# Twelve V columns as six pairs of block products, with two head chains and overlapping scan chunks, in a hybrid Mamba-2 and dilated-attention block

## The chip, the cores and the metric

The kernel runs on one core of a Trainium2 chip. The metric is device time in microseconds (us) of one execution; the figure given for a kernel is the median of its runs. TensorE (PE) multiplies, VectorE (DVE), ScalarE (ACT) and GpSimd (POOL) do the elementwise work, and all transfers are issued by SyncE (SP), one after the other. Each engine takes its own instructions in order.

## The reference

One layer over x of 1024 tokens by 1024 features:

```python
h = rmsnorm(x, norm_mix);  proj = h @ w_in          # z, xBC, dt, q/k/v, gate logits
y_ssm = mamba2_branch(z, xBC, dt, ...) @ w_ssm_out  # conv, silu, chunked scan: 32 heads in 4 groups, 8 chunks of 128
q, k = rope(q), rope(k)                             # 12 heads of 128, three patterns with strides 1, 4, 16
y_att = dilated_attention_branch(q, k, v) @ w_att_out   # softmax over the window, then over the three patterns
x = x + (sigmoid(g0) * y_ssm + sigmoid(g1) * y_att) @ w_mix_out
h = rmsnorm(x, norm_ffn)
x = x + (silu(h @ w_gate) * (h @ w_up)) @ w_down
return rmsnorm(x, norm_final)
```

In the scan a chunk's output needs the state that all chunks before it in its group leave; chunks of one group follow one another by that state alone. A head's attention output is divided and weighted only when the statistics of its three patterns are there.

## The kernel before, in words

**Numbers.** Every large product is made in float32 accuracy out of three float32r matmuls (`mm3`: high by high, high by low, low by high), each of 128x128 weights by 512 columns. A weight tile is loaded raw, ACT casts its high part, DVE subtracts for the low part.

**First stretch (to about 495 us).** z, x, B and C columns of `w_in` (40 columns of 128) are computed in pairs. A pair is a 2x2 block product, done with seven block products instead of eight (class `Seven`, object `A`): `prep` forms sums of weight blocks on POOL and splits each of the seven operands (`split`: ACT copy, DVE subtraction, 128x512); `unit` runs 7 x 4 x 3 = 84 matmuls; `chain` adds the products up on DVE (seven additions of 128x512 from PSUM) and hands two columns to their tasks (`xs_task`, `z_task`, ...), which write DRAM. The list `flat` merges "heavy" pairs (x, B and C: a convolution on DVE) with "light" ones (z).

**Second stretch (495 to about 1165 us).** The other columns go one by one (`direct`, `unit_a`): 2 x 8 x 3 = 48 matmuls, one weight split of 128x1024. They are 36 columns, k, q and v of 12 heads, then gates. Between these matmuls a recorded list of tasks puts the scan and the attention: `chunk(g, c)` for 4 groups by 8 chunks, `head_bg` for 12 heads, one after the other (`att_bg`), `quarter_task` after each two chunks (it writes the scan's output, sums squares with two one-column matmuls and so frees the slab that held X), and `q_load`, which brings X, Z and BC of the next two chunks from DRAM into three slabs of the pool `ssd` (six slabs: two quarters). In `q_load` BC is the last of the three and takes the slab that the quarter before last frees last. `combine(sp)` weights the outputs of six heads.

**Order.** `Pace` is a clock inside the builder: it holds a cost for each instruction and spreads the tasks' instructions among the PE stream when it takes their inputs to be due. It fixes the order on every engine; on the chip an instruction that comes too early in that order stalls its engine.

**Third stretch (from 1165 us).** With `merge` fired, the last five gates, then output projections (`mx_unit`), mixing, the FFN (again with `Seven`) and the down product. The change leaves it as it is, but for where two slabs and the scan's outputs come from.

Of the kernel before, what the change touches and what calls it, by code (L numbers as in the profile page):

```python
# [11 lines left out]
F32 = mybir.dt.float32  # L12
# [44 lines left out]
N_WTS = 7  # L57
N_BRIDGE = 3
N_FLAT_GATES = 0
N_SSD = 6  # L60
SLACK = 4.5
# [272 lines left out]
def hybrid_block(ctx, tc, x, norm_mix, w_in, b_gate, conv_w, conv_b, dt_bias, a_log, d_skip, ssm_norm,  # L334
# [126 lines left out]
    bc_d = [dr.tile([P, 4, 3, 256], F32, name=f"bc_d{g}") for g in range(NG)]  # L461
    b12_d = [dr.tile([P, 4, 512], F32, name=f"b12_d{i}") for i in range(2)]
# [353 lines left out]
    def chunk(g, c):  # L816
# [23 lines left out]
        if c > 0:  # L840
            eb = halves.get([P, 512])
            pair = ea_d[r0:r0 + HG, :].rearrange("(f e) l -> e f l", e=2)
            for e in range(2):
                nc.sync.dma_start(f4(eb.v)[e * 64:(e + 1) * 64], pair[e].partition_broadcast(64))
# [9 lines left out]
        nc.gpsimd.tensor_tensor(f4(y.v), xT, dcol[:, g * 4:(g + 1) * 4].unsqueeze(2).to_broadcast([P, 4, P]), ALU.mult)  # L854
        for h in range(HG):
            gh = g * HG + h
            nc.scalar.activation(E[:, h, :], E[:, h, :], AF.Relu, bias=dtv["acs"][:, c, gh:gh + 1], scale=-1.0)
        nc.scalar.activation(E, E, AF.Exp, scale=-1.0)
# [10 lines left out]
        if not last:  # L869
            yield [xw]  # L870
            yield from bank.room()
            pst = bank.get([P, 512])
            mm(pst.v, Btok, xw.v, True, True)
            xw.free()
            yield [pst, Sn]
            if c == 0:
                nc.vector.tensor_copy(Sn.v, pst.v)
            else:
                nc.vector.tensor_tensor(Sn.v, Sn.v, pst.v, ALU.add)
            pst.free()  # L880
        yield [E]
        nc.vector.tensor_tensor(E, E, cbm.unsqueeze(1).to_broadcast([P, HG, P]), ALU.mult)
        if c > 0:
            yield from bank.room()
            po = bank.get([P, 512])
            for f in range(4):
                fs = slice(f * P, (f + 1) * P)
                mm(po.v[:, fs], G["S"].v[:, fs], CT, True, True)
            G["S"].free()
# [32 lines left out]
    def quarter_task(g, q):  # L922
# [24 lines left out]
        yield [rs]  # L947
        yield from bank.room()
        yield from halves.room()
        pr, rT = bank.get([NCH, P]), halves.get([NCH, P])  # L950
# [6 lines left out]
        rT.free()  # L957
        pace.fire(f"ssd{g}")
# [99 lines left out]
    def rope_task(which, head, r, ps):  # L1058
# [5 lines left out]
        yield from slabs.room(3 if which else 2)  # L1064
        if which:
            att["U", head] = slabs.get([P, S])
# [21 lines left out]
    def v_task(head, r, ps):  # L1088
        yield from slabs.room(2)
        t, V = slabs.get([P, S]), slabs.get([P, 8, P])  # L1090
# [14 lines left out]
        att["v", head] = V  # L1105
        pace.fire(f"v{head}")

    def head_bg(sp, gi, i):
# [3 lines left out]
        yield f"v{head}"  # L1112
        yield [att[0, head], att[1, head], att["v", head]]
        q, k, v = att[0, head].v, att[1, head].v, att["v", head].v
        r = STRIDE[gi]
        if i == 0:
# [6 lines left out]
        for b0 in range(0, 8, step):  # L1123
            yield from bank.room()
            yield from halves.room()
            ps, scb = bank.get([P, 512]), halves.get([P, 512])
            sc = scb.v
# [32 lines left out]
            yield [sc]  # L1160
            yield from bank.room()
            yield from halves.room()
            pt, pT = bank.get([P, 512]), halves.get([P, 512])
# [6 lines left out]
            yield [pT]  # L1170
# [18 lines left out]
        for t in (att[0, head], att[1, head], att["v", head]):  # L1189
            t.free()  # L1190

    def stats_out(sp, gi):
# [7 lines left out]
        att["T", sp, gi] = tt  # L1200
        yield from bank.room()
        yield from halves.room()
        pt, sT = bank.get([32, P]), halves.get([32, P])
# [18 lines left out]
    def combine(sp):  # L1222
# [33 lines left out]
        for i in range(2):  # L1256
            slot = sp * 2 + i
            us = [att["U", gi * 4 + slot] for gi in range(3)]
            for gi in range(3):
                yield from eslabs.room()  # L1260
                fb = eslabs.get([P, S])
                nc.sync.dma_start(fb.v, fd[gi * 2 + i].partition_broadcast(P))
                yield [fb]
                eng = nc.gpsimd if gi < 2 else nc.vector
                eng.tensor_tensor(us[gi].v, us[gi].v, fb.v, ALU.mult)
                fb.free()
            yield [us[0], us[2]]
            nc.vector.tensor_tensor(us[0].v, us[0].v, us[2].v, ALU.add)
            us[2].free()
            yield [us[0], us[1]]  # L1270
            nc.vector.tensor_tensor(us[0].v, us[0].v, us[1].v, ALU.add)
            us[1].free()
            yield [us[0]]
            nc.sync.dma_start(att_d[slot], us[0].v)
            us[0].free()
        pace.fire(f"att{sp}")

    def att_bg():
        for sp in range(2):
            for gi in range(3):  # L1280
                for i in range(2):
                    yield from head_bg(sp, gi, i)
                pace.spawn(stats_out(sp, gi))
            pace.spawn(combine(sp))
# [37 lines left out]
    def direct(*a):  # L1322
# [3 lines left out]
        def run(ps=None, ths=(0, 1)):  # L1326
            ps = unit_a(lids, ps, ths)
            if 1 in ths:
# [6 lines left out]
    units = [direct(kind, gi, head) for sp in range(2) for gi in range(3)  # L1335
             for head in (gi * 4 + sp * 2, gi * 4 + sp * 2 + 1) for kind in "kqv"]
# [792 lines left out]
```

## Time and profile before

| | |
|---|---|
| runs | 2197.47, 2199.08, 2405.64 us; median 2199.08 |
| profiled execution | 2199.41 us, its span 2197.6 us |
| PE busy | 2146.8 us (98%), weight loads 1770.6 us (81%) |
| DVE, ACT, POOL busy | 1502.6 (68%), 885.9 (40%), 631.5 us (29%) |
| transferred | 299.83 MB, 136 GB/s on average |
| granted PE clock | 0.994 over the span |

How to read it: an engine's busy time says how much it did, not whether anybody waited for it. Where PE is busy all through a window, only its own work and its own waits set the time there; what the other engines do counts when PE's idle time names them. A matmul's row shows a modelled duration longer than the distance to the next start, so PE's rate is read from start to start.

### The profile page before, as it was taken

The page shows a single profiled execution, that of the slowest core. Times are in us where ns is not written, and L with a number is a line of the kernel's source. Part 1 is how long each engine was busy: PE and PEld are TensorE (multiplying, and loading weights), DVE is VectorE, ACT ScalarE, POOL GpSimd, SP SyncE. Part 2 cuts the span into 40 slices and gives each one's busy share as a digit, 9 for nine tenths or more (in the row PEclk, how much of TensorE's full clock was granted, in tenths as well). Part 3 has the DMA queues.
Part 4 walks back from the last instruction along what each step waited for, and adds up shares of the span by engine and source line. Part 5 has one row for each costly group of instructions (what it writes and reads, how often), then busy time and mean ns, then how long its engine had stood idle before and what let it go on. Part 6 is the DMA issues. An engine that isn't in the chain of part 4 may idle for free. (4 is left out here: it accounts for less than half of the span.)

```text
span 2197.6 us, 27736 instructions
## 1 busy us (share of the span) xinstructions
PE 2146.8 (98%) x10428; PEld 1770.6 (81%) x10428; DVE 1502.6 (68%) x2050; ACT 885.9 (40%) x1590; POOL 631.5 (29%) x406
## 2 busy tenths in 40 slices
PE   6999999999999999999999999999999999999996
PEld 6788878888888888888888887888778888888885
DVE  6698988885667777744424347644897777767787
ACT  4543443445555565443323224322333333324444
POOL 1332332213544544511012003001454544420002
PEclk9999999999999999999999999999999999999998
DMA  3534243446555554521246467364132323349332
GB/s 128 165 97 123 77 138 106 129 130 201 180 154 167 166 164 153 170 73 39 49 145 213 135 199 237 110 190 127 44 109 95 122 92 115 106 153 336 119 96 101
DMA packets 302602, 299.83 MB, mean 136 GB/s; under 512 B 20036, under 2 KB 246276, under 8 KB 302212
## 3 DMA queue, kind: packets, MB, share of 16 engines
q1 hardware_dynamic: 302468, 298.06, 43.5%
q8 instruction: 82, 1.34, 0.3%
q14 instruction: 52, 0.43, 0.1%
HBM read 225.00 MB, written 73.01 MB: 136 GB/s over the span
## 5 line engine op out<-in xcount | busy, mean ns | idle before, releaser
L166 POOL TENSOR_TENSOR xr<-xr,nfin 128x512 f32<-128x512 f32 x16 | 21.7, 1366 | 185.1 <-ACT jk L166 131.2
L166 POOL TENSOR_TENSOR slab__28_12063<-h2hi,h2lo 128x1024 f32<-128x1024 f32 x1 | 2.4, 2389 | 136.0 <-PE wide__54_11701 L166 136.0
L166 POOL TENSOR_TENSOR slab__26_10566<-slab__26_10566,last__2_10549 128x1024 f32<-128x1024 f32 x1 | 2.4, 2395 | 131.5 <-DMA slab__26_10566<-yt_d 131.5
L166 POOL TENSOR_TENSOR more__3_12059<-h2hi,h2lo 128x512 f32<-128x512 f32 x2 | 2.6, 1294 | 62.3 <-DVE h2lo L166 62.3
L166 POOL TENSOR_TENSOR slab__2_4015<-slab__2_4015,slab__3_4012 128x1024 f32<-128x1024 f32 x1 | 2.4, 2397 | 59.8 <-DMA slab__3_4012<-in_rope 59.8
L166 ACT ACTIVATE jk<-xr 128x512 f32<-128x512 f32 x16 | 10.1, 632 | 15.4 <-DVE xr L166 11.2
L166 POOL TENSOR_TENSOR slab__6_7169<-slab__6_7169,slab__30_9323 128x1024 f32<-128x1024 f32 x1 | 2.4, 2392 | 45.0 <-DMA slab__30_9323<-fd 45.0
L166 POOL TENSOR_TENSOR slab__2_620<-slab__2_618 128x512 f32<-128x512 f32 x1 | 4.0, 3991 | 37.6 <-DMA slab__2_618<-in_w_in 37.6
L166 PE MATMUL wide__1_184<-hhi,slab__1_248 128*128 128x256 f32 (+1 forms) x24 | 8.8, 367 | 2.6 <-ACT hhi L166 2.6
L166 PE MATMUL wide__1_184<-hlo,slab__1_248 128*128 128x256 f32 (+1 forms) x24 | 8.9, 371 | 2.3 <-DVE hlo L166 2.3
L166 DVE TENSOR_TENSOR slab__23_8663<-slab__23_8663,slab__31_9353 128x1024 f32<-128x1024 f32 x1 | 1.2, 1224 | 14.2 <-DMA slab__31_9353<-fd 14.2
L166 POOL TENSOR_TENSOR slab__53_15458<-slab__22_15150,slab__53_15271 128x512 f32<-128x512 f32 x1 | 1.3, 1305 | 32.1 <-DVE slab__53_15271 L166 32.1
L166 ACT ACTIVATE xr<-xr,or 128x512 f32<-128x512 f32 x8 | 5.6, 716 | 11.3 <-DVE or L166 11.3
L166 POOL TENSOR_TENSOR slab__1_596<-hhi,hlo 128x1024 f32<-128x1024 f32 x1 | 2.4, 2406 | 26.7 <-DVE hlo L166 26.7
L166 POOL TENSOR_TENSOR slab__9_8393<-slab__9_8393,slab__3_4012 128x1024 f32<-128x1024 f32 x1 | 2.4, 2403 | 26.5 <-ACT slab__9_8393 L166 26.5
L166 POOL TENSOR_TENSOR slab__21_8664<-slab__21_8664,slab__3_4012 128x1024 f32<-128x1024 f32 x1 | 2.4, 2393 | 25.6 <-ACT slab__21_8664 L166 25.6
L166 POOL TENSOR_TENSOR slab__11_8945<-slab__11_8945,slab__3_4012 128x1024 f32<-128x1024 f32 x1 | 2.4, 2391 | 24.6 <-ACT slab__11_8945 L166 24.6
L166 DVE TENSOR_TENSOR slab__33_9977<-slab__33_9947,slab__61_9976 128x512 fp32r<-128x512 f32 x1 | 0.7, 694 | 12.6 <-PE wide__45_9931 L166 12.6
L166 DVE TENSOR_TENSOR hlo<-slab__1_600,hhi 128x1024 fp32r<-128x1024 f32 x1 | 1.2, 1226 | 11.9 <-DMA slab__3_882<-in_w_in 11.9
L166 PE MATMUL bank__1_186<-ident 128*128 128x128 f32 x36 | 5.9, 343 | 2.7 <-DMA ident<-in_consts 2.7
L166 PEld LDWEIGHTS wide__1_184<-hhi,slab__1_248 128*128 128x128 f32 x24 | 5.3, 219 | 3.9 <-ACT hhi L166 3.7
L166 PEld LDWEIGHTS wide__1_184<-hlo,slab__1_248 128*128 128x128 f32 x24 | 5.3, 219 | 3.9 <-DVE hlo L166 3.8
(7646 smaller groups left out, 8262.7 us busy)
## 6 DMA issues: line engine op xcount, KB each, us to landing
xr<-x_d SPq DMA_DIRECT2D x8, 512.0 KB, 6.4
out<-xr SPq DMA_DIRECT2D x16, 256.0 KB, 2.1
b_d<-hhi SPq DMA_DIRECT2D x1, 1024.0 KB, 5.2
b_d<-hlo SPq DMA_DIRECT2D x1, 1024.0 KB
slab__1_150<-in_x SPq DMA_DIRECT2D x1, 512.0 KB, 3.8
slab__1_151<-in_x SPq DMA_DIRECT2D x1, 512.0 KB
slab__1_158<-in_norm_mix SPq DMA_DIRECT2D x1, 512.0 KB
slab__1_165<-in_w_in SPq DMA_DIRECT2D x1, 512.0 KB, 7.3
```

What stands on the lines that cost most here:

```text
L166: r = call(*args, **kw)
```

## The change

Six parts, in one edit:

1. The 12 V columns leave the list of single columns and become six light pairs of the first stretch (26 pairs instead of 20). `v_task` works in the pool `own`, and V goes to DRAM (`v_d`); `v_load` brings it back when its head starts.
2. Two chains of heads run side by side (`att_bg(0)`, `att_bg(1)`); a head's output U goes to DRAM (`u_d`) at its end, except for the last two, and `slot_bg` reads three of them back when the weights are there.
3. `chunk` asks for E late, takes fewer buffers at once, and starts the next chunk as soon as the state is updated, before its own output is finished.
4. Nine of the eleven gates follow the 24 k and q columns as fillers; two come after `merge` (five before).
5. The weight pool has six slabs instead of seven in the second stretch.
6. The scan's outputs are loaded from slabs as they come free (`y_load`, `spare`) instead of from the `ssd` pool and after `merge`.

```diff
+    v_d = [dr.tile([P, 8, P], F32, name=f"v_d{i}") for i in range(12)]
+    u_d = [dr.tile([P, S], F32, name=f"u_d{i}") for i in range(12)]
...
     def chunk(g, c):
...
-        yield [E, X, BC]
-        yield from halves.room(5)
-        y, xd = halves.get([P, 512]), halves.get([P, 512])
+        yield from halves.room(1 if last else 3)
+        xd = halves.get([P, 512])
         if not last:
             xw, Sn = halves.get([P, 512]), halves.get([P, 512])
...
+        yield [X, BC]
         yield from bank.room()
         pcb = bank.get([P, P])
         mm(pcb.v, BT, CT, True, True)
...
+        yield from halves.room(2 if c else 1)
+        y = halves.get([P, 512])
...
+        if not last:
+            G["S"] = Sn
+            pace.spawn(chunk(g, c + 1))
+        elif g + 1 < NG:
+            pace.spawn(chunk(g + 1, 0))
+        yield [E]
+        for h in range(HG):
...
-        if not last:
-            G["S"] = Sn
-            pace.spawn(chunk(g, c + 1))
-        elif g + 1 < NG:
-            pace.spawn(chunk(g + 1, 0))
         yield [E, xd]
...
     def v_task(head, r, ps):
-        yield from slabs.room(2)
-        t, V = slabs.get([P, S]), slabs.get([P, 8, P])
+        yield from own.room(2)
+        t, V = own.get([P, S]), own.get([P, 8, P])
...
-        att["v", head] = V
-        pace.fire(f"v{head}")
+        yield [V]
+        nc.sync.dma_start(v_d[head], V.v)
+        V.free()
+
+    def v_load(head):
+        yield from slabs.room()
+        t = att["v", head] = slabs.get([P, 8, P])
+        nc.sync.dma_start(t.v, v_d[head])
...
+        if (sp, gi) != (1, 2):
+            yield [att["U", head]]
+            nc.sync.dma_start(u_d[head], U)
+            att["U", head].free()
+        pace.fire(f"u{head}")
...
+    def slot_bg(sp, i):
...
+        for gi in range(3):
+            yield f"u{gi * 4 + slot}"
...
+            us.append(slabs.get([P, S]))
+            nc.sync.dma_start(us[gi].v, u_d[gi * 4 + slot])
+        yield f"fd{sp}"
+        for gi in range(3):
+            yield from slabs.room()
+            fb.append(slabs.get([P, S]))
+            nc.sync.dma_start(fb[gi].v, att["fd", sp][gi * 2 + i].partition_broadcast(P))
+        for gi in range(3):
+            yield [us[gi], fb[gi]]
+            eng = nc.gpsimd if gi < 1 else nc.vector
+            eng.tensor_tensor(us[gi].v, us[gi].v, fb[gi].v, ALU.mult)
+            fb[gi].free()
...
-    units = [direct(kind, gi, head) for sp in range(2) for gi in range(3)
-             for head in (gi * 4 + sp * 2, gi * 4 + sp * 2 + 1) for kind in "kqv"]
-    gates = [direct("gate", i) for i in range(2 + N_BRIDGE + N_FLAT_GATES, 16)]
+    columns = [(kind, gi, head) for sp in range(2) for gi in range(3)
+               for head in (gi * 4 + sp * 2, gi * 4 + sp * 2 + 1) for kind in "kq"]
+    gates = [("gate", i) for i in range(2 + N_BRIDGE + N_FLAT_GATES, 16)]
+    for i in range(len(gates) - N_LAST):
+        columns.insert(FIRST_GATE + i * GATE_STEP, gates.pop(0))
+    units, gates = [direct(*c) for c in columns], [direct(*c) for c in gates]
...
+    light += [(("v", h // 4, h), ("v", h // 4, h + 1)) for h in range(0, 12, 2)]
...
-            wts.pieces.extend(slabs.pieces.popleft() for _ in range(N_WTS))
+            wts.pieces.extend(slabs.pieces.popleft() for _ in range(N_WTS_B))
...
-    pace.spawn(att_bg())
+    for i in range(2):
+        pace.spawn(att_bg(i))
...
-    for u in units:
-        u()
-    while not pace.events.issuperset(("att1", "y01")):
-        if len(gates) > 5:
-            gates.pop(0)()
-        else:
-            pace.idle()
+    while units:
+        next_unit()
+    while not pace.events.issuperset(("fd1", "ssd3")):
+        pace.idle()
```

The diff does not say where `Pace` then puts things. Two places matter.

**PE, from the end of a quarter to the next quarter's first product.** The two one-column matmuls (`128x1`) are the quarter's sums of squares and the last reader of X's slab; the load of the next BC into that slab may go only then. The next chunk's first matmul reads that BC (`slab2__18_4431` before, `slab2__19_5515` now). Before, in group 0:

```order
L166 MATMUL bank2__49_4423<-slab7__1_143,slab2__17_4019 128x1 x2
L166 MATMUL bank3__49_4427<-half4__2_4382,slab18__3_4029 128x512
L166 MATMUL wide1__23_4202<-hhi_147,slab21__15_4058 128x512
L166 MATMUL wide1__23_4202<-hlo_148,slab21__15_4058 128x512
L166 MATMUL wide1__23_4202<-hhi_147,slab10__16_4059 128x512
L166 MATMUL wide1__23_4202<-hhi_147,slab21__15_4058 128x512
L166 MATMUL wide1__23_4202<-hlo_148,slab21__15_4058 128x512
L166 MATMUL wide1__23_4202<-hhi_147,slab10__16_4059 128x512
L166 MATMUL bank1__52_4444<-slab18__3_4029,half0__2_4295 128x128 x4
L166 MATMUL bank0__49_4328<-half7__2_4408,slab25__3_4212 128x128 x4
L166 MATMUL bank2__50_4455<-slab4__18_4378,half9__2_4381 64x128 x8
L166 MATMUL bank3__50_4473<-slab2__18_4431 128x128
```

and now, the corresponding place:

```order
L169 MATMUL bank3__63_5502<-slab7__1_167,slab2__18_5038 128x1 x2
L169 MATMUL bank0__68_5508<-slab15__3_5051,half6__2_5243 128x128 x4
L169 MATMUL wide0__30_5419<-hhi_171,slab12__21_5293 128x512
L169 MATMUL wide0__30_5419<-hlo_172,slab12__21_5293 128x512
L169 MATMUL wide0__30_5419<-hhi_171,slab27__20_5294 128x512
L169 MATMUL wide0__30_5419<-hhi_171,slab12__21_5293 128x512
L169 MATMUL wide0__30_5419<-hlo_172,slab12__21_5293 128x512
L169 MATMUL wide0__30_5419<-hhi_171,slab27__20_5294 128x512
L169 MATMUL bank2__67_5535<-slab5__20_5375,half2__2_5377 64x128 x8
L169 MATMUL bank1__69_5545<-ident_163,half4__3_5454 128x128 x4
L169 MATMUL bank3__64_5550<-slab2__19_5515 128x128
```

Between the sums and the matmul that reads BC stood a 128x512 float32 matmul, six matmuls of a column, eight of 128x128 and eight of 64x128; now a float32 matmul and four of the 128x128 are gone and four transposes (`ident`) have come in.

**SP, at the start of the second stretch.** `in_w_in` is a column's weights, `in_rope` the two rotation tables, then X, Z and BC of the first quarter; the bracket names the semaphores that the transfer waits for. Before:

```order
L166 DMA slab23__17_4008<-in_w_in 128x8x128 [waits DMAHW6_49,DMAHW5_49,Activation_49]
L166 DMA slab19__3_4010<-in_rope 128x1024 [waits PE_49]
L166 DMA slab16__3_4012<-in_rope 128x1024 [waits DMAHW7_49,PE_49]
L166 DMA slab2__17_4019<-xq_d0_117 128x1024 [waits DMAHW0_49,PE_49]
L166 DMA slab1__14_4020<-zq_d0_121 128x1024 [waits DMAHW1_49,PE_49]
L166 DMA slab11__15_4021<-bc_d0_125 128x768 [waits DMAHW2_49,PE_49]
```

and now:

```order
L169 DMA v_d11_140<-own0__24_4948 128x1024 [waits DMAHW4_49,Activation_49]
L169 DMA slab12__20_5028<-in_w_in 128x8x128 [waits DMAHW5_49,PE_49]
L169 DMA slab18__3_5030<-in_rope 128x1024 [waits DMAHW6_49]
L169 DMA slab19__3_5032<-in_rope 128x1024 [waits DMAHW7_49]
L169 DMA slab2__18_5038<-xq_d0_117 128x1024 [waits DMAHW0_49]
L169 DMA slab28__20_5039<-zq_d0_121 128x1024 [waits DMAHW1_49]
L169 DMA slab10__21_5040<-bc_d0_125 128x768 [waits DMAHW2_49]
```

The weight load ahead of the tables waited for ACT and for two transfers; now it waits for a transfer and for PE, and the matmul it waits for is the last one of the stretch's first column. The tables and the first quarter stand behind it.

## Rows read from the trace of the kernel before

**Rows 1.** The page, part 1: busy us (share of the span) xinstructions of each engine.

```profile
PE 2146.8 (98%) x10428; PEld 1770.6 (81%) x10428; DVE 1502.6 (68%) x2050; ACT 885.9 (40%) x1590; POOL 631.5 (29%) x406
```

**Rows 2.** Busy time by window: window, its length, busy us (xinstructions), clock, DMA share, GB/s.

```profile
60.00:495.00 435.00, 432.23 (x1925) 354.83 (x1924) 371.81 (x452) 185.65 (x282) 117.90 (x80) 1.00 0.40 121
495.00:1116.00 621.00, 619.72 (x3565) 510.92 (x3565) 382.32 (x549) 307.05 (x665) 227.71 (x150) 1.00 0.45 136
1165.00:2145.00 980.00, 967.56 (x4324) 799.49 (x4323) 655.85 (x819) 328.77 (x534) 251.09 (x152) 1.00 0.45 143
165.00:330.00 165.00, 162.23 (x729) 133.37 (x728) 147.70 (x188) 68.52 (x109) 47.91 (x35) 1.00 0.37 113
```

**Rows 3.** PE's waits over the whole span: us in total, times, longest us.

```profile
PE bank__23_2264 L166 <- DVE own__7_2108 L166: 1.6, 1, 1.6
...
PE bank__106_7798 L166 <- DVE slab__6_7169 L166: 0.8, 1, 0.8
```

**Rows 4.** Timeline of PE: start us, duration us, operation; 22 matmuls apart.

```profile
497.78 0.39 PE L166 MATMUL wide__22_3931<-hhi,slab__15_3830 128*128 128x512 f32 x1
...
502.77 0.39 PE L166 MATMUL wide__22_4001<-hhi,slab__13_3874 128*128 128x512 f32 x1
```

**Rows 5.** Timelines of DVE, ACT and POOL: one of each kind that the change adds.

```profile
489.90 0.68 DVE L166 TENSOR_TENSOR own__15_3866<-bank__42_3881,own__13_3777 128x512 f32<-128x512 f32 x1
485.12 1.22 DVE L166 TENSOR_TENSOR slab__15_3875<-slab__16_3795,slab__13_3874 128x1024 fp32r<-128x1024 f32 x1
474.84 0.59 ACT L166 COPY own__13_3777<-bank__43_3785 128x512 f32<-128x512 f32 x1 [3.50 <-PE bank__43_3785 L166]
```

**Rows 6.** Timeline of PE and SP between a quarter's sums and BC's first reader.

```profile
549.47 0.32 SPq L166 DMA_DIRECT2D slab__18_4431<-bc_d  x1
548.90 0.50 PE L166 MATMUL bank__49_4423<-slab__1_143,slab__17_4019 128*128 128x1 f32 x4
551.59 1.05 PE L166 MATMUL bank__52_4444<-slab__3_4029,half__2_4295 128*128 128x128 f32 x8
552.48 1.06 PE L166 MATMUL bank__49_4328<-half__2_4408,slab__3_4212 128*128 128x128 f32 x8
553.46 1.09 PE L166 MATMUL bank__50_4455<-slab__18_4378,half__2_4381 128*64 128x128 f32 x16
554.49 0.49 PE L166 MATMUL bank__50_4473<-slab__18_4431 128*128 128x128 f32 x2
554.81 0.60 PE L166 MATMUL bank__53_4475<-ident,slab__16_4429 128*128 128x128 f32 x4
555.36 1.13 PE L166 MATMUL bank__51_4494<-slab__3_4068,slab__3_4161 128*128 128x256 f32 x4
```

**Rows 7.** Tiles of three BC loads (at 549.5, 667.9 and 820.8 us): issue to landing.

```profile
DMA to landing us min/median/max: 3.3/3.3/3.3
DMA to landing us min/median/max: 6.5/6.5/6.5
DMA to landing us min/median/max: 7.6/7.6/7.6
```

**Rows 8.** Transfers issued from 495 to 505 us: KB each, us from issue to landing.

```profile
slab__3_4012<-in_rope SPq DMA_DIRECT2D x1, 512.0 KB, 6.1
...
slab__14_4020<-zq_d SPq DMA_DIRECT2D x1, 512.0 KB, 7.6
```

**Rows 9.** Timeline of POOL: the first rotation.

```profile
505.27 2.40 POOL L166 TENSOR_TENSOR slab__2_4015<-slab__2_4015,slab__3_4012 128x1024 f32<-128x1024 f32 x1 [59.79 <-DMA slab__3_4012<-in_rope]
```

**Rows 10.** Timeline of POOL and DVE at 614 to 619 us: both at once.

```profile
614.25 2.38 POOL L166 TENSOR_TENSOR slab__18_5025<-slab__18_5025,slab__3_4012 128x1024 f32<-128x1024 f32 x1
615.35 0.68 DVE L166 TENSOR_TENSOR half__5_4909<-half__5_4909,bank__60_5036 128x512 f32<-128x512 f32 x1
616.59 1.29 POOL L166 TENSOR_TENSOR slab__16_4838<-half__5_4909,slab__16_4838 128x512 f32<-128x512 f32 x1
616.89 2.07 DVE L166 TENSOR_TENSOR slab__21_4965<-slab__21_4965,cbm 128x1024 f32<-128x1024 f32 x1
```

More of the change, by code (lines that the diff above doesn't have):

```diff
@@ L60 @@
 N_SSD = 6
+N_SPARE = 7
+N_LAST, FIRST_GATE, GATE_STEP = 2, 24, 1
 SLACK = 4.5
@@ L957, in quarter_task @@
         rT.free()
+        if g == NG - 1:
+            slabs.pieces.extend(list(ssd.pieces) + list(eslabs.pieces))
         pace.fire(f"ssd{g}")
@@ L1063, in rope_task @@
                 nc.sync.dma_start(rp[i].v, rope[:, i, :])
-        yield from slabs.room(3 if which else 2)
-        if which:
-            att["U", head] = slabs.get([P, S])
+        yield from slabs.room(2)
         sw = slabs.get([P, S])
@@ L1111, in head_bg @@
         yield f"qk1_{head}"
-        yield f"v{head}"
-        yield [att[0, head], att[1, head], att["v", head]]
+        yield from v_load(head)
+        yield from slabs.room()
+        att["U", head] = slabs.get([P, S])
+        yield [att[0, head], att[1, head]]
         q, k, v = att[0, head].v, att[1, head].v, att["v", head].v
         r = STRIDE[gi]
-        if i == 0:
+        if ("st", sp, gi) not in att:
             att["st", sp, gi] = hfp.tile([P, 2, 2, 8], F32, tag="st", name=f"st{sp}{gi}", bufs=4)
@@ L1169, in head_bg @@
             scb.free()
-            yield [pT]
+            yield [pT, att["v", head]]
             if b0 % 4 == 0:
@@ L1255, in combine @@
         yield [fd]
[L1256 to L1275, printed above, removed]
@@ L1279, in att_bg @@
+    def att_bg(i):
         for sp in range(2):
             for gi in range(3):
[L1281 to L1284, printed above, removed]
+                yield from head_bg(sp, gi, i)
+                if not once(("att", sp, gi)):
+                    pace.spawn(stats_out(sp, gi))
+                    if gi == 2:
+                        pace.spawn(combine(sp))
+                        for j in range(2):
+                            pace.spawn(slot_bg(sp, j))
+                        if sp:
+                            pace.fire("heads")
@@ L1586, in hybrid_block, with spare @@
     yraw, yscale, ysp = {}, {}, {}
+    def spare(n):
+        while "merge" not in pace.events and (slabs.line or len(slabs.pieces) < n + N_SPARE):
+            yield 0.5
     def y_load(th):
@@ L1592, in y_load @@
                 yield f"y{th}{kk - 3}"
-            early = th == 0 and kk < 2
-            yield "ssd3" if early else "merge"
             g, f0 = kk // 2, (kk % 2) * 2
+            for ev in (f"ssd{g}",) if kk < 8 else (f"sl{kk * 2 - 16}", f"sl{kk * 2 - 15}"):
+                yield ev
+            if th == 0:
+                yield "heads"
+                yield from spare(2)
+            else:
+                yield "merge"
             if kk < 8 and kk % 2 == 0:
-                yield from halves.room()
-                yscale[th, g] = halves.get([P, 512])
+                place = slabs if th == 0 else halves
+                yield from place.room()
+                yscale[th, g] = place.get([P, 512])
                 nc.sync.dma_start(yscale[th, g].v, rs_d[g].rearrange("c l -> (c l)")[ts_].partition_broadcast(P))
-            src = ssd if early else slabs
-            yield from src.room()
-            raw = yraw[th, kk] = src.get([P, 2, 512])
+            yield from slabs.room()
+            raw = yraw[th, kk] = slabs.get([P, 2, 512])
             for i in range(2):
@@ L1620, in y_task @@
                     rsb.free()
-            dst = ssd if th == 0 and kk < 2 else slabs
-            yield from dst.room(2)
-            hi, lo = (dst.get([P, 2, 512], F32R) for _ in range(2))
+            if th == 0:
+                yield from spare(2)
+            yield from slabs.room(2)
+            hi, lo = (slabs.get([P, 2, 512], F32R) for _ in range(2))
             yield [raw]
@@ L1664, in hybrid_block @@
     halves = Store([Slot(hfp, f"last{i}", 512) for i in range(2)])
-    slabs.pieces.extend(list(eslabs.pieces) + list(ssd.pieces))
-    ssd.pieces = slabs.pieces
+    wts.pieces.extend(slabs.pieces.popleft() for _ in range(N_WTS - N_WTS_B))
     mplans = []
```

73 lines of the change are left out of this document (49 added, 24 removed).

## The prediction

> **What bounds the kernel now.** I read the page's busy times first: PE is at work for 98% of the span, the next engine, DVE, for 68% [rows 1]. Then the windows [rows 2], because a share of the span mixes stages: in the first stretch (60 to 495 us) PE stood idle for 435 - 432.23 = 2.8 us, in the stretch with scan and attention (495 to 1116 us) for 1.3 of 621 us, in the third for 12.4 of 980. Then the list of PE's waits: in the scan's stretch it names one of 0.8 us as the longest, in the first stretch one of 1.6 us on DVE [rows 3]. So PE's own instructions set the time nearly everywhere, and what DVE, ACT, POOL and the transfers do is hidden. A change gains what it takes out of PE's stream, and loses what it makes PE wait.
>
> **The price of a matmul.** From 497.78 to 502.77 us PE started 22 column matmuls [rows 4]: 0.2268 us each. The granted clock is 1.00 in these windows, its upper level of 2.4 GHz [rows 2].
>
> **Removed.** Twelve V columns cost 12 x 48 = 576 matmuls as single columns and 6 x 84 = 504 as pairs. 72 x 0.2268 = 16.3 us leave PE's stream, and all of it was on the path. V's transposes, the scan's and the heads' matmuls are the same instructions as before. In the built order the 128x512 float32r matmuls fall from 8,252 to 8,180, so the change does what it says.
>
> **Added in the first stretch, hidden.** Each pair brings DVE seven operand splits and seven additions of 128x512, 14 x 0.68 = 9.5 us [rows 5], and ACT eight copies at 0.59 us besides the V columns' own, against 84 x 0.2268 = 19.1 us of PE. DVE is the fullest helper there: 147.7 of 165 us in its densest part, where PE waited 2.8 us [rows 2]. V pairs load it to half, so they thin it out. Cover: PE itself; if an x pair's convolution came late as before, PE would lose the same 2.8 us. Between 0 and 2.8 us of those waits can go; I take 1.0, since the heavy pairs are as heavy as they were.
>
> **Taken from the second stretch.** Between the first scan matmul and the last head matmul PE's order holds 1,716 column matmuls before and 1,176 now. The stretch of 621 us becomes 621 - 540 x 0.2268 = 498 us, and some 485 without V's 96 transposes (four in 0.55 us, [rows 6]). Scan and heads keep their work. DVE keeps 382.3 us less twelve weight splits at 1.22 [rows 2, 5], plus two multiplications more for the combined heads: about 370 of 485 us, 76% where it was 62%. That is less than the 90% at which it cost PE 2.8 us in 165. So I price DVE's fullness at nothing; PE is the cover, and where DVE is late, the scan's products are late next.
>
> **Transfers.** V out and in again (24 transfers of 512 KB) and ten U out and in (20) add 23 MB to 84 MB in 621 us at a DMA share of 0.45 [rows 2]; 12 V weight tiles and V's writes belong to the first stretch, so the second moves some 95 MB in 485 us, a share near 0.64. Each costs SP about 0.3 to 0.4 us of issue, as in [rows 6]. None of the loads of V and U is late: in PE's order at least 8 us of work lie between the load of a V and its first reader, against 7.6 us for the slowest load in [rows 7].
>
> **A wait that becomes tighter: BC.** The load of a quarter's BC may go only after PE has summed the quarter before the last, and the next chunk's first matmul reads it; PE, in order, stands still until it lands, and all columns behind with it. Before, 554.49 - 549.47 = 5.0 us lay between issue and reader at the tightest place [rows 6], and the load took 3.3 us [rows 7]. Now, at the place that the order shows: four 128x128 matmuls 552.48 - 551.59 = 0.89, six column matmuls 1.36, eight 64x128 matmuls 554.49 - 553.46 = 1.03, four transposes 555.36 - 554.81 = 0.55, together 3.8 us, less 0.2 from the sums' end to SP's issue: 3.6 us. Priced alike, the fourteen reloads have 3.2, 3.4, 3.6, 3.9, 4.7, 5.2, 5.4 and 5.9 us, and six have 8.2 or more. With every landing at 3.3 us the waits sum to 0.1 us, with 6.5 to 16.7, with 7.6 to 25.5 (7.6 less each of the eight). The trace times nine BC loads: six took 3.2 to 3.4 us, three 5.7 to 7.6 [rows 7]. A third of 16.7 is 5.6 us, which I take; the ends are 0.1 and 25.5.
>
> The Trainium skill, "DMA: Bandwidth & Descriptors", section "Anatomy of one DMA", gives a transfer about 2.0 us plus its bytes at 436 GB/s; the 393,216 bytes of BC would land in 2.9 us by it (an estimate), no reload would be late, and the sum would come out 5.6 us lower. No BC landing that the trace times is that short, and the loaded ones are twice as long, so the rows decide.
>
> **The start of the second stretch.** SP's weight load now waits for the end of the first column, with both rotation tables and the first quarter behind it. PE returns to that column's PSUM tile one column later, after 48 x 0.2268 = 10.9 us. By then the second table must land, 6.1 us after its issue [rows 8], POOL must multiply for 2.40 [rows 9] and DVE add for 1.22: 9.7 us and two issues ahead of it. X, Z and BC come behind, Z alone at 7.6 us from its issue [rows 8], with four issues ahead. Nothing to 4 us of waiting; I take 2.
>
> **End of the second stretch and after.** Before, gates filled the time until the last combined heads; now seven columns' worth of matmuls stand between the last head and `merge`, some 70 us, so nothing is taken there. The third stretch keeps its instructions and I keep its 12.4 us of waits.
>
> **Sum.** The profiled execution took 2199.41 us (span 2197.6), 0.3 us above the median of 2199.08. 2199.4 - 16.3 - 1.0 + 5.6 + 2.0 = 2189.7: I predict **2190 us**, a gain of 0.4%.
>
> **Rivals.**
> - *Clean* (chance 0.22). The BC loads land early, as six of nine did, and nothing else waits: 2199.4 - 16.3 = 2183, and 2180 if the first stretch's waits go too. For it: PE's order before was as tight as 5.0 us without one wait on a transfer. Against it: eight reloads now have less than 6 us, and the transfers around them are denser.
> - *Slower than before* (0.20). The same loads land late, because 23 MB more share the queues: with all at 7.6 us and the slow start 2199.4 - 16.3 + 25.5 + 4 = 2213. It turns the sign once landings average about 6.2 us, where the waits of the eight sum to 14.3 us and the start adds 2. For it: three of nine landings lay at 5.7 to 7.6 us. Against: those were issued close behind X and Z, while the tight ones go alone after a wait.
> - *DVE shut out by POOL* (0.05). At 616.89 us a DVE operation of 128x1024 on SBUF took 2.07 us beside a POOL operation, where its kind takes 1.22 [rows 5, 10]. If all of POOL's 227.7 us [rows 2] kept DVE out, DVE would need 370 + 228 = 598 us in a stretch of 485, and PE would wait some 113 us: 2199.4 - 16.3 + 113 = 2296. It decides where the overlap adds over 115 us to DVE. Against: the 0.68 us operation at 615.35, with one operand in PSUM, ran at its usual length beside POOL [rows 5, 10], and the overlap as it was is already in the 382.3 us. The Trainium skill, "SBUF — State Buffer", section "SBUF: two separate sides", states this rule: one port pair of DVE and GpSimd is an exclusive lock for operations with two SBUF inputs. The row at 616.89 agrees with it, the one at 615.35 with its limit.
> - *More waits vanish than the change adds* (0.03): 2180 less part of the third stretch's 12.4 us.
>
> The forecast has what is left, 0.50, for 2184 to 2199. Range: 2179 to 2212, from the clean case to the slow one's price; outside lie DVE's rival, the far end of the slow case and the last one, under 0.2. Two per cent, about what a measurement of this kernel can tell from no change, is 44 us. To gain that, nearly all of PE's 50.8 us of idle time [rows 1] would have to go besides: 0.02. To lose it takes DVE's rival or the BC waits twice over: 0.06. Within 2%: 0.92.
>
> **What would show it.** PE's instructions fall by 72 and its busy time by some 16 us. In PE's waits, lines of a one-chunk product (128x128, reading a slab loaded from `bc_d`) on DMA, at most eight, 1 to 4 us each, are the step on BC; their absence makes the clean case. A wait of up to 4 us near the stretch's first scan product is the step on SP. A first stretch some 125 us longer, with DVE's share lower, shows the cover. I am wrong if PE's idle time in the scan's stretch is over 16 us, or if its waits there name DVE rather than transfers.

## The result and the profile after

The changed kernel took 2188.82 us, the median of five runs (2183.57 to 2189.07); the kernel before, run beside it, 2200.82. One of its five runs, 2405.64 us, was a slow one and is left out of the ratio. The ratio is 0.9943, 95% interval 0.9926 to 0.9959: some 12 us faster, clear of the noise and far below 2%. The profiled execution took 2188.89 us, span 2187.1, 10.5 us less than the one before. The forecast of 2190 holds as a number; of its working, three terms do not.

The page's busy times, as in [rows 1]:

```profile
PE 2136.4 (98%) x10356; PEld 1764.4 (81%) x10356; DVE 1559.2 (71%) x2126; ACT 903.6 (41%) x1626; POOL 656.9 (30%) x426
```

The windows that answer to [rows 2], same columns: first stretch, scan's stretch, third stretch, and the start:

```profile
60.00:620.00 560.00, 557.88 (x2516) 459.84 (x2516) 436.83 (x538) 238.97 (x362) 154.53 (x104) 1.00 0.38 117
620.00:1110.00 490.00, 485.48 (x2922) 400.62 (x2921) 367.56 (x533) 269.97 (x619) 214.18 (x146) 0.99 0.59 186
1155.00:2135.00 980.00, 969.54 (x4328) 801.30 (x4327) 652.34 (x821) 329.01 (x532) 243.31 (x149) 1.00 0.45 142
...
0.00:60.00 60.00, 43.48 (x241) 37.21 (x241) 34.27 (x66) 28.52 (x45) 9.60 (x8) 0.86 0.40 125
```

PE has 72 instructions fewer. The first stretch is 125 us longer with a thinner DVE (78% where it was 85%), as forecast. PE's idle time there fell from 2.8 to 2.1 us and in the third stretch from 12.4 to 10.5; in the scan's stretch it rose from 1.3 to 4.5. PE's waits in that stretch are three (in total, times, longest us), and they name DVE, no transfer:

```profile
PE bank__67_5421 L169 <- DVE cbm L169: 2.2, 1, 2.2
PE wide__35_7344 L169 <- DVE slab__6_7342 L169: 1.7, 1, 1.7
PE wide__30_5419 L169 <- DVE slab__3_5413 L169: 0.4, 1, 0.4
```

The first of them in the timelines of ACT, DVE and PE:

```profile
674.16 2.02 ACT L169 COPY slab__3_5391<-wide__29_5286 64x1024 f32<-64x1024 f32 x2 [3.94 <-PE wide__29_5286 L169]
676.22 1.23 DVE L169 TENSOR_TENSOR wide__29_5286<-wide__29_5286,slab__3_5030 128x1024 f32<-128x1024 f32 x1 [3.17 <-ACT slab__3_5391 L169]
677.36 0.28 DVE L169 TENSOR_TENSOR cbm<-bank__66_5380,slab__1_167 128x128 f32<-128x128 f32 x1
677.56 1.21 DVE L169 TENSOR_TENSOR slab__3_5413<-wide__29_5109,slab__3_5299 128x1024 f32<-128x1024 f32 x1
677.78 0.63 PE L169 MATMUL bank__67_5421<-ident,half__3_5313 128*128 128x128 f32 x4 [2.20 <-DVE cbm L169]
678.82 0.80 PE L169 MATMUL wide__30_5419<-hhi,slab__21_5293 128*128 128x512 f32 x1 [0.41 <-DVE slab__3_5413 L169]
679.42 0.63 PE L169 MATMUL wide__30_5419<-hlo,slab__21_5293 128*128 128x512 f32 x1
679.84 0.63 PE L169 MATMUL wide__30_5419<-hhi,slab__20_5294 128*128 128x512 f32 x1
```

DVE is not busy here: it stands idle for 3.17 us. The rotation's multiplication of a new column (`wide__29_5286`) is at the head of its queue and waits until ACT has copied that column's halves. Behind it stand `cbm`, which frees the PSUM bank that PE's transposes take next, and the addition that finishes the column before (`wide__29_5109`) and frees its PSUM tile for PE's next column. The second wait, at 881.19, has the same picture:

```profile
866.93 1.23 DVE L169 TENSOR_TENSOR wide__34_7017<-wide__34_7017,slab__3_5030 128x1024 f32<-128x1024 f32 x1 [0.83 <-ACT slab__4_7227 L169]
866.97 2.36 POOL L169 TENSOR_TENSOR slab__4_7227<-slab__4_7227,slab__3_5032 128x1024 f32<-128x1024 f32 x1 [2.78 <-ACT slab__4_7227 L169]
880.44 1.23 DVE L169 TENSOR_TENSOR wide__34_7214<-wide__34_7214,slab__3_5030 128x1024 f32<-128x1024 f32 x1 [0.33 <-ACT slab__5_7338 L169]
881.58 1.22 DVE L169 TENSOR_TENSOR slab__6_7342<-wide__34_7017,slab__4_7227 128x1024 f32<-128x1024 f32 x1
882.94 0.59 PE L169 MATMUL wide__35_7344<-hhi,slab__25_7221 128*128 128x512 f32 x1 [1.75 <-DVE slab__6_7342 L169]
```

Column 7017 was multiplied at 866.93, POOL was done at 869.33, and the addition came at 881.58, 12 us late, behind the next column's multiplication. Among the 24 rotations DVE's timeline has two such crossings, and they are the two waits; before it has none.

The waits cost more than their length. Behind each, PE's 128x512 matmuls started 0.43 us apart (679.42 to 679.84), about half the speed of [rows 4]: the granted clock was at its lower level, 1.2 GHz, for them (the windows are shown in the last section). Six slow starts after the first wait lost 1.4 us against 0.2268 each, seven after the second 1.4.

**Where the 10.5 us come from.** 72 matmuls: -16.3. Idle time of PE in gaps over 0.12 us: 34.3 before, 33.8 now: -0.4. The clock: outside these gaps, half of PE's time at 1.2 GHz counts as lost (an estimate, from 0.43 us a start beside 0.2268). That is 3.7 us before and 6.8 now in the first 60 us (granted clock 0.91 and 0.86), and 1.7 and 8.3 us after them: +3.1 and +6.6. Over the span the mean granted clock was 0.994 before and is 0.989 now. The sum is -7.0. The other 3.5 us are matmuls of 128x512 that, at the upper level, started 0.2315 us apart on average where they had 0.2319, over 8,235 of them; why is open.

### The profile page after: what moved, and what is told of

Same layout as the page of the kernel before. It is cut to its first block, busy times and chain, and to the rows that moved or that the text cites. A ratio compares the mean times of both kernels' runs of the same rounds, so it can differ in the third digit from the quotient of the medians.

```text
span 2187.1 us, 27856 instructions
## 1 busy us (share of the span) xinstructions
PE 2136.4 (98%) x10356; PEld 1764.4 (81%) x10356; DVE 1559.2 (71%) x2126; ACT 903.6 (41%) x1626; POOL 656.9 (30%) x426
## 5 line engine op out<-in xcount | busy, mean ns | idle before, releaser
L169 POOL TENSOR_TENSOR slab__29_10800<-slab__29_10800,last__1_10783 128x1024 f32<-128x1024 f32 x1 | 2.4, 2396 | 116.1 <-DMA slab__29_10800<-yt_d 116.1
L169 POOL TENSOR_TENSOR slab__3_5034<-slab__3_5034,slab__3_5032 128x1024 f32<-128x1024 f32 x1 | 2.4, 2396 | 69.2 <-DMA slab__3_5032<-in_rope 69.2
L169 ACT ACTIVATE jk<-xr 128x512 f32<-128x512 f32 x16 | 10.1, 632 | 15.4 <-DVE xr L169 11.2
L169 PE MATMUL wide__1_208<-hhi,slab__1_272 128*128 128x256 f32 (+1 forms) x24 | 9.7, 403 | 2.2 <-ACT hhi L169 2.2
L169 POOL TENSOR_TENSOR slab__14_10033<-slab__14_10033,slab__10_9841 128x1024 f32<-128x1024 f32 x1 | 2.5, 2505 | 26.2 <-DMA slab__14_10033<-yt_d 26.2
L169 PE MATMUL wide__35_7344<-hhi,slab__25_7221 128*128 128x512 f32 x16 | 7.5, 466 | 1.7 <-DVE slab__6_7342 L169 1.7
L169 PE MATMUL wide__1_208<-hhi,slab__1_273 128*128 128x256 f32 (+1 forms) x24 | 8.8, 365 | 0.0
L169 PE MATMUL wide__30_5419<-hhi,slab__21_5293 128*128 128x512 f32 x16 | 8.0, 497 | 0.4 <-DVE slab__3_5413 L169 0.4
L169 POOL TENSOR_TENSOR slab__9_9508<-slab__9_9508,slab__4_9506 128x1024 f32<-128x1024 f32 x1 | 2.4, 2431 | 19.6 <-DMA slab__9_9508<-yt_d 19.6
```

Of the source, the lines that this page charges most:

```text
L169: r = call(*args, **kw)
```

## Experiments

Two theories on the waits. *Queue*: an instruction that stands too early in DVE's order blocks those behind it, and how full DVE is does not matter. *Load*: DVE's 75% of the stretch (367.56 of 490 us) makes the waits, the places are chance. The runs of the kernel before that stood beside the experiments had medians of 2201.0 to 2203.1.

**E1. The multiplication later.**

```diff
-        nc.vector.tensor_tensor(ps.v, ps.v, rp[0].v, ALU.mult)
         yield [sw]
+        nc.vector.tensor_tensor(ps.v, ps.v, rp[0].v, ALU.mult)
         nc.gpsimd.tensor_tensor(sw.v, sw.v, rp[1].v, ALU.mult)
```

> The rotation's multiply on DVE is issued only after ACT's two copies are due, so it no longer stands in DVE's queue while ACT still copies. In the changed kernel PE waited 2.2 us and 0.4 us at 676 to 679 us and 1.75 us at 881 us, and after each its 128x512 matmuls started 0.43 us apart instead of 0.23 for 7 starts (1.5 us lost each). Queue theory (these waits come from two places where DVE's order puts the next column's multiply ahead of this column's addition): both places are gone from the order, so about 4.4 us of waits and 3.0 us of slow matmuls go, and the time is 2181 to 2185, unless a new place appears. Load theory (DVE at 75% of the stretch is too full, the places are chance): DVE's work is the same, the waits appear elsewhere, 2187 to 2190.

Measured: 2185.40 us (2182.00 to 2187.19), ratio 0.9927 (0.9913 to 0.9940). The crossings and their waits are gone, and others came in their place, the longest 0.7 us:

```profile
PE wide__37_8066 L169 <- DVE slab__8_8062 L169: 0.7, 1, 0.7
...
```

PE idles for 3.7 of the 490 us from 620 to 1110, where it had 4.5. The time lies at the edge of what the queue theory gave; its interval overlaps that of the change, so the gain of 3 us is not shown by this run alone (see E12).

**E2. The planner's price of POOL.**

```diff
-                s += (e - s) * (0.55 if kind == "dve" else 1.0)
+                s += (e - s) * (0.55 if kind == "dve" else 0.0)
```

> The planner's price of a POOL operation beside DVE is cut: it added all of DVE's overlapping time to POOL's (at the place of the 1.75 us wait it took POOL's rotation to be ready 8.4 us after its issue, where the trace has 2.4), now it adds none. Every order of DVE, POOL and PE shifts a little. Queue theory: the additions stand close behind POOL's multiplications, no addition is behind the next column's multiply, PE's waits in the scan's stretch fall from 4.4 us to under 1.5 and the time to 2181 to 2186. Load theory: same work on every engine, 2187 to 2190. If the price was right for the first and third stretches, whose order it also sets, new waits there make it 2190 or more.

Measured: 2186.12 us, ratio 0.9934 (0.9921 to 0.9947). No crossing is left, yet PE still idles for 4.6 of the 490 us, in pieces of up to 1.6. The queue theory's 1.5 us is missed; on the time the run is inconclusive.

**E3. E1 and E2 together.**

> Both edits of the two runs before. Queue theory: no further gain over the better of the two, 2181 to 2185, with no PE wait on DVE over 1 us between 620 and 1110 us. Load theory: 2187 to 2190 with waits of 3 us or more there.

Measured: 2188.72 us, ratio 0.9941 (0.9929 to 0.9954): no gain, against the queue theory as I had put it. No crossing is in its order. A 3.0 us wait on an addition stands in the scan's stretch without a crossing, and one of 6.2 us in the third stretch where the change has 3.3. Here PE also waits for a BC, 0.9 and 0.3 us. A new order brings new places.

**E4. V columns one by one again.** `light` loses the pairs, `columns` runs over "kqv", `v_task` takes `slabs`, `v_load` waits for the column's write, and the nine gates follow 36 columns instead of 24; all else is the change's.

```diff
-    light += [(("v", h // 4, h), ("v", h // 4, h + 1)) for h in range(0, 12, 2)]
...
-               for head in (gi * 4 + sp * 2, gi * 4 + sp * 2 + 1) for kind in "kq"]
+               for head in (gi * 4 + sp * 2, gi * 4 + sp * 2 + 1) for kind in "kqv"]
```

> Of the change only the pairs of V columns are undone: the twelve V columns are computed one by one in the second stretch again (and still go through DRAM), everything else stays. PE gets its 72 matmuls back: 72 x 0.2268 = 16.3 us. If the pairs are the whole gain and the waits in the scan's stretch stay, 2188.8 + 16.3 = 2205. If those waits (4.4 us and 3.0 us of slow matmuls) come from the shorter stretch, they go, and it is 2198. If the gain came from the other parts of the change (two chains, overlapping chunks) and the pairs gave nothing: 2189.

Measured: 2213.08 us (2205.57 to 2214.47), ratio 1.0048 (1.0030 to 1.0066): 24 us slower than the change, and slower than the kernel before. 16.3 us are the 72 matmuls; PE's idle time (span less busy) is 57.1 us where the change has 50.7, 6.4 more, its longest new waits 3.1 us on the load of a V, 2.8 us on a rotation's addition (a crossing) and 1.6 us on a BC. So without the pairs there is no gain; the other five parts, with V as it is here, cost some 11 us. V's way through DRAM, which this run keeps, adds the 3.1 us wait, so the 11 us hold for this order alone.

**E5. One chain of heads.**

```diff
-                yield from head_bg(sp, gi, i)
-                if not once(("att", sp, gi)):
+                yield from head_bg(sp, gi, 0)
+                yield from head_bg(sp, gi, 1)
+                if True:
...
-    for i in range(2):
-        pace.spawn(att_bg(i))
+    pace.spawn(att_bg(0))
```

> The two chains of heads are put back into one, V pairs and all else stay. In the kernel before, twelve heads one after the other took from 501 to some 1,080 us, 48 us each, with 36 columns around them. If one chain needs that again, it ends 12 x 48 = 576 us after 641, at 1217, where two chains end at 1091 and the fillers last to 1155: some 62 us of PE without work, 2250 us. Rival: a head was paced by its columns before; the fastest heads of the changed kernel took 49 us side by side, a head alone could take half, the chain still ends by 1110: 2187 to 2192.

Measured: 2248.93 us, ratio 1.0211 (1.0194 to 1.0228), the time of the first theory, but only in part by its way. PE's idle time rises by 41 us (span less busy, 92.0 where it was 50.7); the clock takes the rest. By windows (620 to 1050, the scan's end, after the last filler) it idles for 19.8, 10.6 and 11.1 us:

```profile
620.00:1050.00 430.00, 410.19 (x2464) 334.47 (x2462) 309.88 (x447) 229.23 (x508) 202.72 (x139) 0.98 0.59 184
1050.00:1110.00 60.00, 49.37 (x233) 40.97 (x234) 40.97 (x47) 18.51 (x34) 14.59 (x7) 0.86 0.41 139
...
1210.00:1260.00 50.00, 38.89 (x156) 30.22 (x154) 36.53 (x38) 17.00 (x31) 24.93 (x9) 0.90 0.84 283
```

Only the last lies after the fillers, as the first theory had all 62 us; three crossings stand in the first.

**E6. No overlap of chunks.** The block that starts the next chunk stands ahead of `yield [E, xd]` again.

> Only the overlap of scan chunks is undone: a chunk starts the next one where it did before, after its own last state product is added. Before, 30 chunks took 386 us, 12.9 us each; in the changed kernel 31 take 438, 14.1 each, with the last product at 1089 and fillers until 1155. Queue theory: at 12.9 us the scan of 32 chunks still fits (413 us), nothing changes: 2186 to 2191. Rival (the two head chains take PSUM banks and DVE, so that a chunk without overlap takes longer than in the kernel before): at 17 us it ends at 1195, 40 us after the fillers, 2229.

Measured: 2219.82 us, ratio 1.0077 (1.0062 to 1.0092): the rival. The scan's last product moved from 1089.55 to

```profile
1199.92 1.97 PE L169 MATMUL bank__133_9929<-slab__34_9877,half__21_9879 128*64 128x128 f32 x16 [5.03 <-DVE slab__34_9877 L169]
```

17.8 us a chunk. That a chunk took 12.9 in the kernel before was no measure for it here; that the two chains of heads are the reason is the rival's argument, and no run tests it by itself. PE idles for 17.0 us from 1160 to 1220, where the fillers are out. Part of the 31 us are two crossings that this order has (the longer wait 6.0 us, to 931.87).

**E7. Four gates paired too**, with E1's edit and `N_FLAT_GATES = 4`.

> The first edit (rotation's multiply later), and four gates move from the second stretch's fillers into the first stretch as two more pairs. PE's work falls by 2 x 12 x 0.2268 = 5.4 us, its fillers by four columns, 44 us of the 66 that lie between the last head's product (1089) and the end of the fillers (1155). Theory that a pair is worth its matmuls while fillers cover the scan and heads: 2185.4 - 5.4 = 2180. Rival: the cover is used up, PE waits for the last combined heads, and each of the 5.4 us is lost again or more: 2186 to 2200.

Measured: 2185.10 us, ratio 0.9919 (0.9904 to 0.9934). PE has 24 instructions fewer, 5.4 us, and all of it is lost again against E1: PE idles for 54.6 us (span less busy) where E1 has 50.8, among it 2.2 us for ACT amid the scan and 3.7 us in four waits of one column at the start of the third stretch.

**E8. BC loaded twice.**

```diff
             nc.sync.dma_start(b.v[:, :m], d[g][:, q])
+            if d is bc_d:
+                nc.sync.real.dma_start(b.v[:, :m], d[g][:, q])
```

> Every load of BC is issued twice in a row (the order of all else is that of the changed kernel), so BC is in its slab later by one issue (0.32 us) and one more transfer of 393,216 bytes (about 1 us at the 400 GB/s that the busiest slices show). The changed kernel's tightest reloads had 3.55, 3.76, 3.94 and 4.84 us from issue to reader and landed after 3.1 to 3.6. If tight reloads land early because nothing else is in flight, they now land after about 4.5, and PE shows three waits on BC of 0.5 to 1.0 us, 2 us in all: 2189 to 2193. If they had more slack than that (landings that the trace shows are upper bounds), no wait: 2187 to 2190. If the queue is the limit, as my prediction's 5.6 us assumed, waits of 2 to 4 us at several places: 2195 or more.

Measured: 2218.18 us, ratio 1.0067 (1.0052 to 1.0082), 29 us slower than the change. My expectation had the second copy wrong: SP issues it only after the first has landed (the seven first copies whose landing the trace has landed 0.01 to 0.02 us before), so a BC comes twice as late. SP's rows therefore time all sixteen landings, by the distance of the two issues:

```profile
692.74 0.32 SPq L169 DMA_DIRECT2D slab__19_5517<-bc_d  x1
695.84 0.32 SPq L813 DMA_DIRECT2D slab__19_5517<-bc_d  x1
...
1040.00 0.75 SPq L169 DMA_DIRECT2D slab__25_8678<-bc_d  x1
1049.08 0.32 SPq L813 DMA_DIRECT2D slab__25_8678<-bc_d  x1
```

Seven landed after 3.1 to 3.2 us, the others after 3.8 to 9.1. PE's waits are of the kind that the prediction looked for, 15.4 us in six (a seventh has 0.3). One of the six, 3.0 us, is for the stretch's first BC, which is no reload:

```profile
PE bank__91_6556 L169 <- DMA slab__21_6528<-bc_d: 3.2, 1, 3.2
PE bank__61_5102 L169 <- DMA slab__21_5040<-bc_d: 3.0, 1, 3.0
...
```

**E9. Heads' outputs copied by ACT.** `nc.vector.tensor_copy` becomes `nc.scalar.copy` where U leaves PSUM.

> The copies of the heads' outputs out of PSUM (24 of 128x512, 1.12 us each in the changed kernel's trace) go from DVE to ACT: 27 us less for DVE, whose share of the scan's stretch falls from about 75% to 70%. The planner's order moves with it, and now has three places (two in the changed kernel) where DVE's order holds the next column's multiplication ahead of this column's addition. Load theory (DVE's fullness makes the waits): PE's 4.4 us of waits shrink, 2182 to 2187. Queue theory (places make the waits): they stay or grow by a third place's 2 us and its slow matmuls, 2188 to 2194.

Measured: 2209.30 us, ratio 1.0031 (1.0021 to 1.0042). DVE's busy time in the stretch fell to 346.14 us, and PE idled for 18.8 of the 490. The three crossings are there, additions 14.4, 13.8 and 18.8 us after their multiplications; the last in DVE's and PE's timeline:

```profile
956.89 1.23 DVE L169 TENSOR_TENSOR wide__36_7487<-wide__36_7487,slab__3_5030 128x1024 f32<-128x1024 f32 x1 [1.89 <-ACT slab__7_7936 L169]
975.72 1.99 DVE L169 TENSOR_TENSOR slab__26_8069<-wide__36_7487,slab__7_7936 128x1024 f32<-128x1024 f32 x1 [1.10 <-POOL slab__6_7904 L169]
977.76 0.79 PE L169 MATMUL wide__37_8078<-hhi,slab__30_7702 128*128 128x512 f32 x1 [6.57 <-DVE slab__26_8069 L169]
```

Less load on DVE and 20 us more time speak against the load theory; waits of 1.2, 2.2 and 6.6 us stand at the crossings, the rest elsewhere. The run is no clean test: the order moved, and the copies now stand in ACT's queue, whose own part (PE's waits name ACT for 2.0 us) was not told apart.

**E10. More work for DVE.**

```diff
         nc.vector.tensor_tensor(h3(xd.v), tok, bcast(dtv["dt"][:, c, hs]), ALU.mult)
+        for _ in range(2):
+            nc.vector.real.tensor_tensor(h3(xd.v), tok, bcast(dtv["dt"][:, c, hs]), ALU.mult)
```

> Every scan chunk multiplies its input by dt three times instead of once, with the same result, and the planner does not know it: the order of all else is that of the changed kernel. DVE gets 64 x 0.68 = 44 us more in the stretch of some 490 us, from 75% to 84%. My prediction priced DVE's fullness at nothing up to 90%: then 2187 to 2192. If an instruction's place in the queue decides, each chunk's 1.36 us is paid where PE's margin is shorter than that: of 31 chunks a third would cost about 1 us and its slow matmuls, 10 to 20 us: 2199 to 2209. If fullness decides, PE pays what does not fit into DVE's idle quarter: nothing.

Measured: 2195.38 us, ratio 0.9966 (0.9952 to 0.9980): 6.6 us for 42 us of work (409.38 us busy in the stretch), between the two cases. The waits of 2.2 and 1.8 us stand unchanged, new ones of up to 2.5 have come. PE idles for 11.7 us of the 490 where it had 4.5. So more work on DVE is not free, but here costs about a sixth of its own length.

**E11. Two gates paired**, with E1's edit and `N_FLAT_GATES = 2`.

> The first edit (rotation's multiply later) and one more pair of two gates in the first stretch, taken from the fillers. PE's work falls by 12 x 0.2268 = 2.7 us against the first edit alone (2185.4), and 22 us of the 66 us of cover go. Four gates gained nothing more (2185.1), with 4.3 us of waits of a gate's column behind the last heads. If those waits came from the cover being used up, two gates keep enough of it: 2182 to 2184. If the shifted order brings its own waits, 2185 to 2188.

Measured: 2185.47 us, ratio 0.9919 (0.9907 to 0.9932): no gain over E1. So it was not only the cover that ate E7's 5.4 us.

**E12. The change again.**

> The changed kernel once more, in the company of newer runs of the kernel before, to tell whether moving the rotation's multiply gained anything: its five runs took 2183.57 to 2189.07 (median 2188.82), those of the first edit 2182.00 to 2187.19 (2185.4). Queue theory (3 to 4 us came from the two places): ratio to before 0.9935 to 0.9950, median 2187 to 2190, and the same two waits of 2.2 and 1.7 us in the profile. Load theory (the edit gained nothing): ratio 0.992 to 0.993, median near 2185.

Measured: 2187.29 us (2183.30 to 2189.42), ratio 0.9940 (0.9924 to 0.9956), with the same waits of 2.2, 0.4 and 1.7 us. Of the 11 runs of the change 3 lie below 2186.2 us, of the 14 of E1, E7 and E11, which share the first edit, 11 do (medians 2187.7 and 2185.4). So that edit seems worth some 2 us. The intervals of the ratios overlap, and E7 and E11 also have fewer matmuls, so the size is not shown.

## Why the prediction was right, and where it was not

- **72 matmuls, 16.3 us: right.** PE's count says it, and E4 takes them back.
- **First stretch, -1.0: right for the waits, not for the clock.** Of the waits one of 1.8 us is left, and the window's idle time fell from 2.8 to 2.1 us. But behind that wait the clock fell, as it had not before (270 to 290 us in the last section): eight matmuls started 0.43 to 0.48 us apart and lost 1.7 us.
- **BC, +5.6: wrong.** The covers (the time from a BC's issue to its first reader) were about right where they are tight: 3.55, 3.76, 3.94, 4.83 and 5.50 us where I had worked out 3.2, 3.4, 3.6, 3.9 and 4.7. The next three were 6.48, 7.80 and 8.57 us, not 5.2 to 5.9, so that with every landing at 6.5 the waits sum to 11 us and not 16.7. The issues and first readers of the first two and of one with a long cover, and the landings of the three tiles:

```profile
689.62 0.32 SPq L169 DMA_DIRECT2D slab__19_5515<-bc_d  x1
693.38 0.39 PE L169 MATMUL bank__64_5550<-slab__19_5515 128*128 128x128 f32 x2
793.00 0.32 SPq L169 DMA_DIRECT2D slab__21_6522<-bc_d  x1
796.55 0.39 PE L169 MATMUL bank__91_6549<-slab__21_6522 128*128 128x128 f32 x2
1019.13 0.70 SPq L169 DMA_DIRECT2D slab__25_8664<-bc_d  x1
1034.63 0.38 PE L169 MATMUL bank__121_8795<-slab__25_8664 128*128 128x128 f32 x2
```

```profile
DMA to landing us min/median/max: 3.3/3.3/3.3
DMA to landing us min/median/max: 3.3/3.3/3.3
DMA to landing us min/median/max: 9.4/9.4/9.4
```

  The step that failed is "a third of 16.7": it drew landings from [rows 7] as if landing and cover were independent. A tight cover is one where SP had to wait for PE's sums; no load was ahead of that BC, and the four tightest landed in 3.1 to 3.6 us. The three slowest reloads (7.7 to 9.4) went behind other loads and had covers of 8.7 to 15.5 us. The prediction named this argument against its own rival and did not use it in the term. The tightest reload had 0.2 us to spare. In other orders PE did wait for a reload, 0.9 us in E3 and 1.6 us in E4, and not at a tight cover: in E3 the load landed 8.1 us after its issue, and the wait ended 8.3 us after it. The Trainium skill, "DMA: Bandwidth & Descriptors", "Anatomy of one DMA", gave 2.9 us (an estimate) and so no late reload; its figure is a fit for transfers that GpSimd issues, while SP issues these. E8's 3.1 lies near it for a load that goes alone, its 9.1 shows what the rule leaves out.
- **The slower rival: its mechanism was real, its price too small.** E8 puts landings of a BC that goes alone near the 6.5 us for which I had 16.7 us of waits. Its reloads have 12.7, the first BC 3.0, and the time rises by 29: PE's idle time (span less busy) by 24.0, from 50.7 to 74.6 us. Of that 15.7 us name BC and most of the rest DVE; the clock takes the other 5 us.
- **Start of the second stretch, +2.0: wrong, by a margin of 0.8 us.** The second table, issued at 630.84, was there at 636.59, POOL took 2.40, DVE's addition ended at 640.23, and PE came back to the tile at 641.04.
- **DVE's fullness at nothing: the step that failed the other way.** I had written that I would be wrong if the waits named DVE; they do: 4.3 us, with 2.8 us of slow matmuls behind them. The step looked at how full DVE is and not at its order. DVE's work was as priced, 367.56 us where I had about 370, so POOL did not shut it out. At the first wait DVE stood idle for 3.17 us behind one instruction; E1 moved that instruction and both waits went, and E10 added 42 us of work and left them as they were. A busy share says nothing of who stands behind whom; E10 says what more work does cost.
- **The sum** came out right by chance. 7.6 us of transfer waits (BC and the start) did not come. What came instead was not in it: 4.3 us of DVE waits, and 9.7 us of lower clock in the profiled execution. Against these stood 3.5 us of faster starts and 2 us less idle time in the third stretch, which were not in it either.
- **Open:** why the other five parts alone (E4) cost 11 us is told only in part by its waits, which part of E7's and E11's loss is order and which cover was not told apart, nor why the clock fell behind some waits and not behind others.

## What to carry to other kernels

Where one engine's work sets the time, count its instructions first: that term was exact. It is not a gain by itself: E7 and E11 took out 5.4 and 2.7 us more and gained nothing. Then read, for each in-order queue, which instruction waits for something late and who stands behind it; a busy share does not tell it. Price a transfer by the loads that go under the same conditions, not by the mixture of all, and count up to twice its length for a wait of PE of 2 us: the 1.75 us wait cost 1.4 us more in slow matmuls.

## What the runs showed of the hardware

The clock after a wait is not fixed. Around four of PE's waits the granted clock was, in the profile of the change (windows as in [rows 2]):

```profile
270.00:290.00 20.00, 18.16 (x74) 14.48 (x73) 17.70 (x28) 8.16 (x18) 3.31 (x3) 0.91 0.44 139
670.00:690.00 20.00, 17.39 (x105) 13.87 (x104) 13.96 (x21) 10.21 (x24) 9.77 (x7) 0.91 0.54 171
880.00:890.00 10.00, 8.25 (x33) 6.41 (x34) 8.49 (x12) 7.89 (x21) 5.63 (x4) 0.83 0.68 211
1325.00:1345.00 20.00, 16.74 (x67) 13.37 (x66) 16.79 (x16) 9.63 (x18) 5.47 (x2) 0.91 0.47 139
```

in that of E12, the same program with the same waits 1 to 2 us earlier:

```profile
0.00:60.00 60.00, 42.19 (x243) 35.98 (x244) 35.31 (x67) 29.10 (x46) 9.60 (x8) 0.91 0.39 125
670.00:690.00 20.00, 17.39 (x123) 14.11 (x124) 14.50 (x21) 9.88 (x22) 9.79 (x7) 1.00 0.63 201
880.00:890.00 10.00, 9.52 (x51) 8.12 (x52) 8.79 (x14) 6.23 (x14) 7.52 (x7) 1.00 0.51 175
```

and in that of the kernel before, at the waits that answer to the change's first and last:

```profile
270.00:290.00 20.00, 18.36 (x82) 14.84 (x81) 19.39 (x23) 8.04 (x14) 2.07 (x2) 1.00 0.36 106
1335.00:1355.00 20.00, 15.96 (x69) 12.53 (x68) 19.91 (x18) 7.65 (x14) 8.58 (x4) 1.00 0.54 175
```

The same holds for the start, 0.86 and 0.91. The change's runs of 2183 to 2189 us go with it: the fastest of E12's had a mean clock of 0.993, two of the slowest 0.988 and 0.989.
